# A hybrid encoder layer on one core: scheduling priority of the first group's output projection, and the buffer of the last input rows

## The chip, the cores and the metric

One NeuronCore of a Trainium2 chip runs the whole kernel. The metric is the device time of one execution in microseconds (us), and what is compared is the median of several executions. In the profile PE is the matmul engine (TensorE), DVE is VectorE, ACT is ScalarE, POOL is GpSimd and SP is the engine that issues nearly all DMAs. The granted clock of PE is given as a share of full speed: 1.00 is 2.4 GHz and 0.50 is 1.2 GHz.

## The reference

One layer for 1024 prompt rows and 64 sample rows, D = 1024, so 1088 columns in the kernel's transposed layout:

```
h  = RMSNorm(x) @ W_in
x += W_out @ concat[ConformerConv, ForgettingAttn, HGRN2, StickBreaking]
x += MemoryCrossAttn(RMSNorm(x), mem K/V)
x += SquaredReLU-MLP(RMSNorm(x))
y  = RMSNorm(x)
```

The convolution is a depthwise filter of 31 taps over a gated input, followed by a layer norm over its 256 channels and a SiLU. Each mixer gives 256 of the 1024 channels that W_out takes in.

## The kernel before

Every product is made from three matmuls: both factors are split into a high part (`wh`, `ap` written by ACT) and a low part (`wl`, `ap` written by DVE), and high x high, high x low and low x high are added in PSUM (helper line L71; ACT's helper is L74, DVE's split is L171).

**Start.** x comes in nine row tiles (`TT`: eight of 128 prompt rows and one of 64 sample rows), is transposed on PE (`px`, L282) and split, and the rms factor of each column is broadcast into `rb` (products `pr`). Columns are worked in three chunks of 512, 256 and 320. The nine tiles `xt0` to `xt8` wait in SBUF: the first seven have buffers of their own in pool `xa`, and `xt7` and `xt8` borrow buffers of pool `att`, by naming the tag of a later tile. Two tiles with the same tag share buffers, so the later tile's first write waits until the last reader of the earlier one is done. Before the change `xt8` takes the tag `kT` (one buffer). `kT` is also the tile into which DVE writes the first projection, the keys of the stick-breaking attention: `kT<-pm,rb` (L441), one write for each chunk; the values go to `vT` (L447). Their transposes back are `pn` (L365).

**Middle.** Work is written as generators ("lanes": projections, two attentions, convolution, HGRN) that are recorded in turns; each piece carries a priority, and a scheduler orders the instructions of each engine by priority (a smaller number goes first) and by what is ready. The order is fixed when the program is built; at run time each engine runs its list in order and waits where an operand is missing. The priorities are PR_PROJ < PR_ATT < PR_HGRN < PR_CONV < PR_MM < PR_END. The convolution is the filler of DVE: each tap is one DVE instruction (L794, `y<-ext,cwT,y`). Behind its last taps comes its epilogue, in two halves of 183 columns: sums over channels on PE (`pme`), subtraction (L816), squares on ACT (`sq`), sums of squares on PE (`pva`), the rsqrt chain, scale (L825, L826), SiLU (L830), and the write of the result to DRAM (`mix_d<-y`, L832 to L835).

**End of the mixers.** The output projection is `dense_add` (L1107 on; products `pa`): for each of 8 row tiles m of W_out, 8 terms k, three matmuls for each term; then DVE adds the sum to x (L1120). PSUM pool `ps1` has three buffers and the weight pool two. Group 0 is columns 0 to 511 and group 1 is columns 512 to 1087, in two PSUM pieces of 320 and 256. The inputs are the mixers' results, read back from DRAM and split (`split_mix`, L1035: `mix<-mix_d` for group 0, `aq<-mix_d` for group 1). The convolution gives the terms k = 0 and 1, and its last columns belong to group 1 alone. Group 1 takes its terms in the order `MIX = (2, 3, 4, 5, 6, 7, 0, 1)`. After group 0 come `rms_stats` (`pr`) and `rms_apply` (L1096) for the memory attention. All of this is recorded with `tc.cur_priority = PR_END` (L1033), behind every lane.

Of the kernel before, what the change touches and what calls it, by code (L numbers as in the profile page):

```python
# [8 lines left out]
F32 = mybir.dt.float32  # L9
# [8 lines left out]
P = 128  # L18
D = 1024
# [3 lines left out]
T = SP + SS  # L23
# [15 lines left out]
P_COST = 18.0  # L39
PROJ_ORDER = "sb0 h0 sb1 ff cv fox0 h1 fox1 kv".split()  # L40

PR_PROJ, PR_ATT, PR_HGRN, PR_CONV, PR_MM, PR_END = (i * 10 ** 6 for i in (1, 2, 3, 4, 5, 10))


class Need:
# [7 lines left out]
def kernel(ctx: ExitStack, tc: tile.TileContext, *args):  # L53
# [16 lines left out]
    def mm(out, lhsT, rhs, start, stop, **kw):  # L70
        nc.tensor.matmul(out, lhsT=lhsT, rhs=rhs, start=start, stop=stop, **kw)  # L71

    def act(out, in_, func, **kw):
        nc.scalar.activation(out=out, in_=in_, func=func, **kw)  # L74
# [35 lines left out]
    for m in LEVELS[1:]:  # L110
        nb = 64 // m
        f = const.tile([P, nb], F32, name=f"lf{m}", tag="lvlf", bufs=1)
# [27 lines left out]
    def rstd_chain(pool, n, mean_sq, tag, scale=1.0, parts=P, out=None, tiles=None):  # L140

        tags = [tag + c for c in "vyt"] if isinstance(tag, str) else tag
        tags = [dict(tag=g) if isinstance(g, str) else dict(zip(("tag", "bufs"), g)) for g in tags]
        if tiles:
            v, y, t = tiles[0][:, :n], out, tiles[1][:, :n]
        else:
            v, y, t = (out if c == "y" and out is not None else pool.tile([P, n], F32, name="rs" + c, **g)[:parts]
                       for c, g in zip("vyt", tags))
        V.tensor_scalar(out=v, in0=mean_sq, scalar1=scale, scalar2=EPS, op0=ALU.mult, op1=ALU.add)
        act(y, v, AF.Ln)  # L150
        act(y, y, AF.Exp, scale=-0.5)
        V.tensor_tensor(out=t, in0=y, in1=y, op=ALU.mult)
        V.scalar_tensor_tensor(out=t, in0=t, scalar=-0.5, in1=v, op0=ALU.mult, op1=ALU.mult)
        V.scalar_tensor_tensor(out=y, in0=t, scalar=1.5, in1=y, op0=ALU.add, op1=ALU.mult)
        return y
# [21 lines left out]
    def fetch_w(src, r0, kt, c0, cols=P):  # L177
        raw = wp.tile([P, KD, P], F32, name="wr", tag="wr")[:, :kt, :cols]
        nc.sync.dma_start(out=raw, in_=src[r0:r0 + kt * P, c0:c0 + cols].rearrange("(k p) c -> p k c", p=P))
        return raw  # L180
# [51 lines left out]
    def h_at(k, t0, n):  # L232
        g = 0 if t0 < 512 else 1
        t0 -= GR[g][0]
        return hx[g][k][0][:, t0:t0 + n], hx[g][k][1][:, t0:t0 + n]
# [5 lines left out]
    att = mx.enter_context(tc.tile_pool(name="att", bufs=2))  # L241
    wk = mx.enter_context(tc.tile_pool(name="wk", bufs=2))
    rb = wk.tile([P, T], F32, name="rb", tag="rb", bufs=1)
    with ExitStack() as pa:
        xa = pa.enter_context(tc.tile_pool(name="xa", bufs=1))
        ps_a = pa.enter_context(tc.tile_pool(name="ps_a", bufs=4, space=PSUM))
        ss = xa.tile([P, 9], F32, name="ss")
        V.memset(ss, 0.0)
        junk = att.tile([P, 2, D], BF16, name="junk", tag="vn")
        xt = []  # L250
        for i, (t0, n) in enumerate(TT):
            xt.append((att.tile([P, T], F32, name=f"xt{i}", tag=("vn", "kT")[i - 7], bufs=(2, 1)[i - 7])[:, :D] if i >= 7 else
                       xa.tile([P, D], F32, name=f"xt{i}")))
            nc.sync.dma_start(out=xt[i][:n], in_=x_prompt[t0:t0 + n] if i < 8 else x_sample)
            if i in (3, 6):
                c = (C_SK, C_SV)[i // 3 - 1]
                early[c] = fetch_w(w_in, 0, KD, c)

        def stats(c0, cn, tiles):
            for i in tiles:  # L260
                n = TT[i][1]
                if i % 2:
                    V.tensor_tensor_reduce(out=junk[:n, 1], in0=xt[i][:n], in1=xt[i][:n], scale=1.0, scalar=0.0,
                                           op0=ALU.mult, op1=ALU.add, accum_out=ss[:n, i:i + 1])
                else:
                    act(junk[:n, 0], xt[i][:n], AF.Square, accum_out=ss[:n, i:i + 1])
            r = rstd_chain(xa, len(tiles), ss[:, tiles[0]:tiles[0] + len(tiles)], "ra", scale=1.0 / D)
            pr = ps_a.tile([P, 512], F32, name="pr", tag="pr", bufs=1)
            for j, i in enumerate(tiles):
                n = TT[i][1]  # L270
                dg = xa.tile([P, P], F32, name="dg", tag="dg", bufs=2)
                V.tensor_scalar(out=dg[:n, :n], in0=ident[:n, :n], scalar1=r[:n, j:j + 1], scalar2=None, op0=ALU.mult)
                mm(pr[:, j * P:j * P + n], ones[:n], dg[:n, :n], True, True)
            act(rb[:, c0:c0 + cn], pr[:, :cn], AF.Copy)

        for c0, cn in CH:
            tiles = [i for i, (t0, n) in enumerate(TT) if c0 <= t0 < c0 + cn]
            for k in range(KD):
                px = ps_a.tile([P, 512], F32, name="px", tag="px")
                for i in tiles:  # L280
                    t0, n = TT[i]
                    nc.tensor.transpose(px[:, t0 - c0:t0 - c0 + n], xt[i][:n, k * P:(k + 1) * P], ident[:n, :n])  # L282
                hi, lo = h_at(k, c0, cn)
                act(hi, px[:, :cn], AF.Identity, scale=g_mix[:, k:k + 1])
                V.scalar_tensor_tensor(out=lo, in0=px[:, :cn], scalar=g_mix[:, k:k + 1], in1=hi.bitcast(F32),
                                       op0=ALU.mult, op1=ALU.subtract)
                xs = xa.tile([P, 512], F32, name="xs", tag="xs", bufs=4)
                if k % 2:
                    V.tensor_copy(out=xs[:, :cn], in_=px[:, :cn])
                else:  # L290
                    act(xs[:, :cn], px[:, :cn], AF.Copy)
                nc.sync.dma_start(out=xT_d[:, k, c0:c0 + cn], in_=xs[:, :cn])
            stats(c0, cn, tiles)
# [722 lines left out]
    while lanes:  # L1016
# [13 lines left out]
            ln.need = y.key  # L1030
        else:
            ln.t += y * ln.rate
    tc.cur_priority = PR_END  # L1033

    def split_mix(k, src, t0, n, which):  # L1035
        nc.sync.dma_start(out=src, in_=mix_d[k][:, t0:t0 + n])
# [19 lines left out]
    def unit(tag, dt=F32):  # L1056
        return units[tag].tile([P, 576], dt, name=tag, tag=tag)
# [7 lines left out]
    def wide():  # L1065
        return unit("aq")
# [11 lines left out]
    def rms_stats(g, psum, tag, tiles=None, keep=False, s2=None):  # L1078

        if not s2:  # L1080
            for k in range(KD):
                s2 = add_square(g, k, s2, wide())
        rr = unit("tm")
        for c0, cn in GR[g][2]:
            ps = psum.tile([P, 512], F32, name="pr", tag=tag)
            mm(ps[:, :cn], ones, s2[:, c0:c0 + cn], True, True)
            v, t = tiles or (unit("tm"), unit("tm"))
            rstd_chain(None, cn, ps[:, :cn], "xxx", scale=1.0 / D, out=rr[:, c0:c0 + cn], tiles=(v, t))
            if keep:
                V.tensor_tensor(out=t[:, :cn], in0=v[:, :cn], in1=rr[:, c0:c0 + cn], op=ALU.mult)  # L1090
                nc.sync.dma_start(out=rms_d[:, c0:c0 + cn], in_=t[:, :cn])
        return rr
# [7 lines left out]
    def rms_apply(g, gains, rr, which, over=False):  # L1100

        dst = [pair(which) for _ in range(KD)]
        for c0, cn in GR[g][2]:
            for k in range(KD):
                hf = normed(g, k, gains, rr, c0, cn, xT[g][k] if over else None)
                split(dst[k][0][:, c0:c0 + cn], dst[k][1][:, c0:c0 + cn], hf[:, :cn])
        return dst  # L1107

    def dense_add(g, src, r0, kt, a, psum, ahead=None, store=False, after=None, order=None):

        t0, n, _ = GR[g]
        for m in (0, 4, 1, 5, 2, 6, 3, 7) if after else range(KD):
            w = load_w(src, r0, kt, m * P)
            if ahead:
                ahead(m)
            for c0, cn in GR[g][2]:
                ps = psum.tile([P, 512], F32, name="pa", tag="mm")
                mm3(ps[:, :cn], w, lambda k: (a[k][0][:, c0:c0 + cn], a[k][1][:, c0:c0 + cn]), kt, order=order)
                xs = xT[g][m][:, c0:c0 + cn]
                V.tensor_tensor(out=xs, in0=xs, in1=ps[:, :cn], op=ALU.add)  # L1120
            if store:
                nc.sync.dma_start(out=x2_d[m][:, t0:t0 + n], in_=xT[g][m])
            if after:
                tc.cur_priority += 600
                after(m)
                tc.cur_priority -= 600
# [3 lines left out]
    with ExitStack() as pm_:  # L1130
# [94 lines left out]

        MIX = (2, 3, 4, 5, 6, 7, 0, 1)
        dense_add(0, w_out, 0, KD, mix[0], ps1, ahead)
        h2 = rms_apply(0, g_mem, rms_stats(0, ps2, "sc"), 0)
        dense_add(1, w_out, 0, KD, mix[1], ps1, lambda m: load_x(1, m), order=MIX)
        for g in range(2):  # L1230
# [321 lines left out]
```

## Time and profile before

| | |
|---|---|
| median of 3 runs | 1765.38 us (1765.11 to 1768.04) |
| the profiled execution | 1760.05 us, span 1758.3 us, mean granted PE clock 0.991 |
| busy | PE 1694.8, DVE 1172.1, ACT 791.4, POOL 94.1 us |
| chain of work that ended last | PE 75%, DVE 15%, ACT 4%, DMA 3%, issue 2% |

Read the busy times first, then the chain, to see which engine bounds the span; then the stretches around the two edits. The columns of each view are given with its rows below. "[9.11 <-DVE cvo L805]" behind a row means that the engine was idle for 9.11 us before it, and that the instruction that released it was DVE's write of `cvo`.

### The profile page before, as it was taken

The page shows a single profiled execution, that of the slowest core. Times are in us where ns is not written, and L with a number is a line of the kernel's source. Part 1 is how long each engine was busy: PE and PEld are TensorE (multiplying, and loading weights), DVE is VectorE, ACT ScalarE, POOL GpSimd, SP SyncE. Part 2 cuts the span into 40 slices and gives each one's busy share as a digit, 9 for nine tenths or more (in the row PEclk, how much of TensorE's full clock was granted, in tenths as well). Part 3 has the DMA queues.
Part 4 walks back from the last instruction along what each step waited for, and adds up shares of the span by engine and source line. Part 5 has one row for each costly group of instructions (what it writes and reads, how often), then busy time and mean ns, then how long its engine had stood idle before and what let it go on. Part 6 is the DMA issues. An engine that isn't in the chain of part 4 may idle for free.

```text
span 1758.3 us, 29395 instructions
## 1 busy us (share of the span) xinstructions
PE 1694.8 (96%) x11379; PEld 1504.8 (86%) x11379; DVE 1172.1 (67%) x2231; ACT 791.4 (45%) x1614; POOL 94.1 (5%) x201
## 2 busy tenths in 40 slices
PE   6999999999989979999999999999999999999997
PEld 4987768787777768988899989999999999999987
DVE  6266789988986897667777696555556444444435
ACT  6265657547447855346456363433334212122213
POOL 3021111101120200000000000000000000000000
PEclk9999999999999989999999999999999999999999
DMA  8521332242237348232522343333335722332112
GB/s 256 142 80 33 111 87 88 71 123 76 71 95 215 111 140 254 73 97 67 156 78 73 101 124 99 99 106 99 101 105 203 266 94 87 99 100 74 37 37 102
DMA packets 233195, 194.70 MB, mean 111 GB/s; under 512 B 17502, under 2 KB 199711, under 8 KB 233055
## 3 DMA queue, kind: packets, MB, share of 16 engines
q1 hardware_dynamic: 232639, 192.54, 35.6%
q8 instruction: 90, 1.47, 0.4%
q14 instruction: 50, 0.41, 0.1%
q10 hardware_dynamic: 160, 0.26, 0.0%
q0 software_dynamic: 256, 0.01, 0.0%
HBM read 137.96 MB, written 53.72 MB: 109 GB/s over the span
## 4 chain that ended last, share of the span: by engine, by line
PE 75%; DVE 15%; ACT 4%; DMA 3%; issue 2%; POOL 0%; SPq 0%; DVEq 0%; POOLq 0%; ACTq 0%
PE pz L71 24%; PE pw L71 15%; PE pm L71 11%; PE pa L71 9%; PE pq L71 5%; PE z L71 2%; DVE y L794 2%; PE pmo L71 2%; PE pms L71 1%; PE po L71 1%; PE pt L517 1%; PE pv L71 1%; DVE wl L171 1%; DVE hsc L934 1%; DVE sba L494 1%
## 5 line engine op out<-in xcount | busy, mean ns | idle before, releaser
L74 ACT ACTIVATE wh<-wr 128x1024 fp32r<-128x1024 f32 (+1 forms) x179 | 161.4, 909 | 439.6 <-PE pz L71 195.2
L171 DVE TENSOR_TENSOR wl<-wr,wh 128x1024 fp32r<-128x1024 f32 (+1 forms) x179 | 184.3, 1036 | 63.8 <-ACT wh L74 62.5
L71 PE MATMUL pw<-ap,wh 128*128 128x512 f32 x720 | 223.3, 391 | 1.0 <-DVE xt L1120 0.6
L71 PE MATMUL pz<-ap,wh 128*128 128x288 f32 x988 | 198.3, 294 | 0.0
L71 PE MATMUL pa<-ap,wh 128*128 128x256 f32 (+2 forms) x768 | 187.0, 332 | 2.1 <-DVE xt L1120 2.1
L71 PE MATMUL pm<-hx,wh 128*128 128x512 f32 (+1 forms) x640 | 176.6, 363 | 2.1 <-ACT wh L74 1.4
L71 PEld LDWEIGHTS pz<-ap,wh 128*128 128x128 f32 x988 | 161.3, 188 | 4.6
L71 PE MATMUL pm<-ap,wh 128*128 128x256 f32 (+1 forms) x768 | 164.7, 307 | 0.0
L71 PEld LDWEIGHTS pw<-ap,wh 128*128 128x128 f32 x720 | 130.0, 188 | 23.5 <-issue 0.8
L71 PE MATMUL pz<-ap,wl 128*128 128x288 f32 x494 | 145.4, 294 | 0.0
L71 PEld LDWEIGHTS pa<-ap,wh 128*128 128x128 f32 x768 | 132.3, 191 | 12.5 <-DVE xt L1120 2.4
L71 PE MATMUL pw<-ap,wl 128*128 128x512 f32 x360 | 140.3, 390 | 0.0
L71 PEld LDWEIGHTS pm<-hx,wh 128*128 128x128 f32 x640 | 110.2, 192 | 20.6 <-ACT wh L74 2.2
L71 PEld LDWEIGHTS pm<-ap,wh 128*128 128x128 f32 x768 | 123.8, 191 | 4.2 <-issue 1.7
L71 PE MATMUL pa<-ap,wl 128*128 128x512 f32 (+2 forms) x384 | 127.2, 332 | 0.1
L1349 DVE TENSOR_TENSOR xt<-xt,pz 128x576 f32<-128x576 f32 x56 | 42.2, 753 | 115.6 <-PE pz L71 108.8
L71 PE MATMUL pm<-ap,wl 128*128 128x256 f32 (+1 forms) x384 | 114.0, 297 | 0.0
L71 PE MATMUL pm<-hx,wl 128*128 128x512 f32 (+1 forms) x320 | 112.7, 352 | 0.1
L794 DVE SCALAR_TENSOR_TENSOR y<-ext,cwT,y 128x376 f32<-128x376 f32 (+1 forms) x180 | 100.9, 604 | 0.3
L1349 DVE TENSOR_TENSOR xt<-xt,pw 128x512 f32<-128x512 f32 (+2 forms) x80 | 51.0, 638 | 69.8 <-PE pw L71 67.6
L71 PE MATMUL pq<-ap,wh 128*128 128x512 f32 (+2 forms) x384 | 93.0, 331 | 0.0
L71 PEld LDWEIGHTS pz<-ap,wl 128*128 128x128 f32 x494 | 92.7, 188 | 0.0
(385 smaller groups left out, 3572.9 us busy)
## 6 DMA issues: line engine op xcount, KB each, us to landing
wr<-in_w_up_dram SPq DMA_DIRECT2D x32, 512.0 KB, 4.1
wr<-in_w_down_dram SPq DMA_DIRECT2D x32, 512.0 KB, 3.5
wr<-in_w_in_dram SPq DMA_DIRECT2D x24, 512.0 KB, 4.3
hid_d<-ap SPq DMA_DIRECT2D x32, 288.0 KB, 2.4
aq<-hid_d SPq DMA_DIRECT2D x32, 288.0 KB, 3.7
wr<-in_w_out_dram SPq DMA_DIRECT2D x16, 512.0 KB, 4.2
wr<-in_w_mq_dram SPq DMA_DIRECT2D x16, 512.0 KB, 3.8
wr<-in_w_mo_dram SPq DMA_DIRECT2D x32, 256.0 KB, 2.8
```

The lines of the kernel that those rows point to most:

```text
L71: nc.tensor.matmul(out, lhsT=lhsT, rhs=rhs, start=start, stop=stop, **kw)
L74: nc.scalar.activation(out=out, in_=in_, func=func, **kw)
L171: V.tensor_tensor(out=lo, in0=src, in1=hi.bitcast(F32), op=ALU.subtract)
L494: V.tensor_tensor_scan(out=v[:, ::-1], data0=z[:, n - 1:0:-1], data1=v[:, ::-1], initial=-NEG, op0=ALU.add, op1=ALU.subtract)
L517: nc.tensor.transpose(ps[:w, j - jb], p[:, j * P:j * P + w], ident)
L794: V.scalar_tensor_tensor(out=y, in0=ext[:, j:j + n], scalar=cwT[:, ct, j:j + 1], in1=y, op0=ALU.mult, op1=ALU.add)
L934: V.copy_predicated(sc[r, s_at:s_at + ng, :, r].rearrange("p g h (c w) -> p (g h) c w", w=2 * m)[:, :, :, m:], lvl[m][r, par * nb:(par + 1 ...
L1349: eng.tensor_tensor(out=out, in0=a, in1=b, op=ALU.add)
```

## The change

A new priority PR_OUT stands between PR_HGRN and PR_CONV. The loads and splits of the mixers' results, the weight loads of the first projection and `dense_add(0)` itself are recorded at PR_OUT; after `dense_add(0)` the priority goes back to PR_END. And `xt8` takes the tag `q2` (one buffer, used later by the stacked queries of the stick-breaking attention) in the place of `kT`. Lines below the edits move by one or two (L441 becomes L442, L794 L795, L1120 L1121).

```diff
-PR_PROJ, PR_ATT, PR_HGRN, PR_CONV, PR_MM, PR_END = (i * 10 ** 6 for i in (1, 2, 3, 4, 5, 10))
+PR_PROJ, PR_ATT, PR_HGRN, PR_OUT, PR_CONV, PR_MM, PR_END = (i * 10 ** 6 for i in (1, 2, 3, 4, 5, 6, 10))
...
-            xt.append((att.tile([P, T], F32, name=f"xt{i}", tag=("vn", "kT")[i - 7], bufs=(2, 1)[i - 7])[:, :D] if i >= 7 else
-                       xa.tile([P, D], F32, name=f"xt{i}")))
+            xt.append(att.tile([P, T], F32, name="xt7", tag="vn")[:, :D] if i == 7 else
+                      att.tile([P, 2, T], F32, name="xt8", tag="q2", bufs=1)[:, 0, :D] if i == 8 else
+                      xa.tile([P, D], F32, name=f"xt{i}"))
...
-    tc.cur_priority = PR_END
+    tc.cur_priority = PR_OUT
...
         dense_add(0, w_out, 0, KD, mix[0], ps1, ahead)
+        tc.cur_priority = PR_END
         h2 = rms_apply(0, g_mem, rms_stats(0, ps2, "sc"), 0)
```

What this does to the lists of the engines is seen at three places. First, PE where the output projection begins, before the change (`pv` belongs to the last attention, `pa` is dense_add(0), `pme` is the convolution's first sum):

```order
2340 L71 MATMUL pv<-aT,vn 64x128 x5
2341 L71 MATMUL pa<-ap,wh 128x512 x4
2342 L71 MATMUL pme<-y_4800,ones 128x183
2343 L71 MATMUL pme<-y_4816,ones 128x183
2344 L71 MATMUL pa<-ap,wl 128x512
2345 L71 MATMUL pa<-ap,wh 128x512 x2
2346 L71 MATMUL pa<-ap,wl 128x512
2347 L71 MATMUL pva<-sq_5331,ones 128x183
2348 L71 MATMUL pva<-sq_5332,ones 128x183
```

After the change the same sums stand on PE behind the last product of dense_add(0), among the first ones of dense_add(1) (`pa` of 320 columns):

```order
2467 L71 MATMUL pa<-ap,wh 128x512 x2
2468 L71 MATMUL pa<-ap,wl 128x512
2469 L71 MATMUL pme<-y_4800,ones 128x183
2470 L71 MATMUL pme<-y_4816,ones 128x183
2471 L71 MATMUL pa<-ap,wh 128x320 x2
2472 L71 MATMUL pa<-ap,wl 128x320
2473 L71 MATMUL pa<-ap,wh 128x320 x2
2474 L71 MATMUL pa<-ap,wl 128x320
2475 L71 MATMUL pa<-ap,wh 128x320
2476 L71 MATMUL pva<-sq_5331,ones 128x183
2477 L71 MATMUL pva<-sq_5332,ones 128x183
```

All 192 matmuls of dense_add(0) now stand ahead of the convolution's epilogue; the second half's `pme` and `pva` follow at 2482 to 2492.

Second, DVE at the start of that epilogue, after the change (the adds of dense_add(0) are `xt<-xt,pa`):

```order
1014 L1121 TENSOR_TENSOR xt<-xt,pa 128x512
1015 L171 TENSOR_TENSOR wl<-wr,wh 128x1024
1016 L1121 TENSOR_TENSOR xt<-xt,pa 128x512
1017 L817 SCALAR_TENSOR_TENSOR y_4800<-pme,y_4800 128x183
1018 L817 SCALAR_TENSOR_TENSOR y_4816<-pme,y_4816 128x183
1019 L171 TENSOR_TENSOR wl<-wr,wh 128x1024
1020 L149 TENSOR_SCALAR rs<-pva 128x183
```

The epilogue begins behind the last of the eight adds; the taps themselves end at row 1008, between the fourth add and the fifth. Of the instructions between row 1017 and the epilogue's end at row 1045 only row 1019 is not the convolution's.

Third, DVE at the start of the program, before the change and then after it (`ap<-px` and `xs` belong to the transposes of x):

```order
64 L289 COPY xs<-px 128x320
65 L272 TENSOR_SCALAR dg<-ident,rsy 64x64
66 L441 TENSOR_TENSOR kT<-pm,rb 128x512
67 L171 TENSOR_TENSOR kl<-kT,kh 128x512
68 L769 MEMSET ext_3684 128x30
```

```order
45 L286 SCALAR_TENSOR_TENSOR ap<-px,g_mix,ap 128x320
46 L152 TENSOR_TENSOR rst<-rsy 128x2
47 L442 TENSOR_TENSOR kT<-pm,rb 128x512
48 L153 SCALAR_TENSOR_TENSOR rst<-rst,rsv 128x2
49 L448 TENSOR_TENSOR vT<-pm,rb 128x512
```

The first write of `kT` moves from behind the last of x's transposes to ahead of most of the last chunk's. On PE the transposes `pn<-ident,kT` and the products of the second chunk follow it:

```order
98 L283 MATMUL px<-ident,xt_240 128x64
99 L366 MATMUL pn<-ident,kT 128x128 x4
100 L71 MATMUL pm<-ap,wh 128x256 x2
101 L71 MATMUL pm<-ap,wl 128x256
102 L71 MATMUL pm<-ap,wh 128x256 x2
103 L71 MATMUL pm<-ap,wl 128x256
```

Three of the eight `px` of the last chunk now stand behind these products. From PE's instruction 234 to 3095 and from DVE's 88 to 829 the two programs' lists are the same.

## Rows read from the trace of the kernel before

**Rows 1.** The page, part 1: busy us (share of the span) xinstructions of each engine.
```profile
PE 1694.8 (96%) x11379; PEld 1504.8 (86%) x11379; DVE 1172.1 (67%) x2231; ACT 791.4 (45%) x1614; POOL 94.1 (5%) x201
```

**Rows 2.** The page, part 4: the chain that ended last, by engine.
```profile
PE 75%; DVE 15%; ACT 4%; DMA 3%; issue 2%; POOL 0%; SPq 0%; DVEq 0%; POOLq 0%; ACTq 0%
```

**Rows 3.** Stretches: us, busy of PE, PEld, DVE, ACT, POOL; clock, DMA share, GB/s.
```profile
36.00:44.00 8.00, 5.48 (x31) 3.63 (x29) 7.00 (x21) 5.55 (x14) 0.00 (x0) 0.94 0.58 192
44.00:50.00 6.00, 5.47 (x26) 5.09 (x25) 2.03 (x5) 2.15 (x4) 3.03 (x5) 0.51 0.52 151
...
640.00:660.00 20.00, 10.75 (x69) 8.50 (x69) 19.68 (x39) 5.62 (x13) 0.00 (x0) 0.74 0.48 154
```

**Rows 4.** Timeline of PE where the projection begins: start, us, instruction, [idle before].
```profile
643.60 1.20 PE L71 MATMUL pa<-ap,wh 128*128 128x512 f32 x4
653.90 1.59 PE L71 MATMUL pme<-y,ones 128*128 128x183 f32 x4 [9.11 <-DVE cvo L805]
...
659.28 0.78 PE L71 MATMUL pme<-y,ones 128*128 128x183 f32 x4
...
665.13 0.61 PE L71 MATMUL pa<-ap,wh 128*128 128x512 f32 x2
...
665.81 0.61 PE L71 MATMUL pa<-ap,wh 128*128 128x512 f32 x2
```

**Rows 5.** Timeline of DVE: the last taps and the convolution's epilogue.
```profile
641.37 11.82 DVE L794 SCALAR_TENSOR_TENSOR y<-ext,cwT,y 128x366 f32<-128x366 f32 x23
...
666.46 0.34 DVE L152 TENSOR_TENSOR rs<-sq 128x183 f32<-128x183 f32 x1
...
670.24 0.65 DVE L826 TENSOR_SCALAR y<-y,cvec 128x183 f32<-128x183 f32 x2
...
673.73 0.60 DVE L830 TENSOR_TENSOR y<-y,sq 128x183 f32<-128x183 f32 x2
```

**Rows 6.** Timeline of ACT: root and sigmoid of the epilogue, then a split of the last load.
```profile
658.76 0.36 ACT L74 ACTIVATE sq<-rs 128x183 f32<-128x183 f32 x1 [1.72 <-DVE rs L149]
...
662.73 0.70 ACT L74 ACTIVATE sq<-y 128x183 f32<-128x183 f32 x2 [0.79 <-DVE y L826]
663.33 1.08 ACT L74 ACTIVATE sq<-sq 128x183 f32<-128x183 f32 x4
...
680.64 0.67 ACT L74 ACTIVATE ap<-aq 128x576 fp32r<-128x576 f32 x1
```

**Rows 7.** Timeline of SP's queue: the loads behind the epilogue's writes.
```profile
676.97 0.79 SPq L1036 DMA_DIRECT2D aq<-mix_d  x2
```

**Rows 8.** The DMA view: issues, KB each, median us from issue to landing.
```profile
aq<-mix_d SPq DMA_DIRECT2D x8, 288.0 KB, 3.6
```

**Rows 9.** Timeline of PE in dense_add(1): tiles of 320 columns.
```profile
701.70 0.46 PE L71 MATMUL pa<-ap,wh 128*128 128x320 f32 x2
...
702.14 0.46 PE L71 MATMUL pa<-ap,wh 128*128 128x320 f32 x2
```

**Rows 10.** Timeline of PE at the start of the program.
```profile
36.16 0.38 PE L282 MATMUL px<-ident,xt 128*128 128x128 f32 x2
36.38 0.61 PE L71 MATMUL pr<-dg,ones 128*128 128x128 f32 x4
36.92 1.99 PE L282 MATMUL px<-ident,xt 64*128 64x64 f32 x10
...
40.69 1.21 PE L282 MATMUL px<-ident,xt 128*128 128x128 f32 x6 [0.95 <-ACT xs L74]
43.47 1.41 PE L71 MATMUL pr<-dg,ones 128*128 128x128 f32 x4 [1.57 <-DVE dg L272]
...
50.63 0.40 PE L71 MATMUL pm<-ap,wh 128*128 128x256 f32 x2
...
50.99 0.40 PE L71 MATMUL pm<-ap,wh 128*128 128x256 f32 x2
```

**Rows 11.** Timeline of DVE at the start of the program.
```profile
43.89 0.67 DVE L441 TENSOR_TENSOR kT<-pm,rb 128x512 f32<-128x512 f32 x1
```

## The prediction

> **What bounds the kernel now.** I read the busy times first: PE is busy for 1694.8 of 1758.3 us, DVE for 1172.1 [rows 1]. The chain that ended last runs through PE for 75% and DVE for 15% [rows 2]. So the kernel gets shorter only where PE idles or runs at half clock, some 60 us in all, and the next views are stretches with both columns side by side. Two of them belong to the two edits. Between 640 and 660 us PE is busy for 10.75 of 20 us at a clock of 0.74, while DVE is full with 19.68 [rows 3]. Between 36 and 50 us PE is busy for 5.48 of 8 and then 5.47 of 6, the latter at 0.51 [rows 3]. The timelines say what ended each wait. At 643.60 PE starts the output projection with four matmuls, then idles for 9.11 us until DVE has written `cvo` [rows 4]: next in its list stands the convolution's `pme`, DVE is working through 23 taps in 11.82 us [rows 5], and PE cannot pass over an instruction. In the early stretch there are waits of 0.95 and 1.57 us for the evacuation and scaling of x [rows 10], and the first `kT` is written only at 43.89 [rows 11], with most of PE's products in its list behind it.
>
> I work the sum against the profiled execution, 1760.05 us: its span and 1.75 us around it. It lies 5.3 us below the median of the runs, so I carry the difference, not the level, to 1765.38. A measurement of this kernel tells 0.2% from no change, 3.5 us.
>
> **The change, edit B (`xt8` in tag `q2`).** No instruction is added or removed; a false dependency goes. `kT<-pm` moves up in DVE's list, and on PE 36 to 48 products of 256 columns come to stand among the transposes on which it waited. The stretch to judge runs from 36.16, PE's first transpose after the first chunk's values, to 50.63, from where products of 256 columns go at full speed, three in 0.36 us [rows 10]. Up to 50.20, one triple earlier, are 14.0 us. They hold 21 transposes `px`, 10 broadcasts `pr`, 4 `pc`, 8 `pn`, and 12 products of 256 columns. Four `pr` took 0.54 us from start to start [rows 10], 0.13 each, so 43 x 0.13 = 5.6 us; 12 products take 4 x 0.36 = 1.4 us. The content at full clock is 7.0 us and the loss 7.0 us: 3.05 us of idle time (2.52 + 0.53 from the busy columns [rows 3]), the rest half clock and waits inside the transposes (ten `px` took until the next `pr`, 1.9 us, where 1.3 would do). The wait for `xs` on ACT (0.95 us) is not about `kT`; I keep it. Gain 7.0 - 0.95 = **6.0 us**. The bounds: 7.0 if nothing is left; 2.1 if only idle time goes and the half clock stays. I take the value near the top, since products now fill the places of the waits, and the half clock stands only behind the stretch where PE was mostly idle (the granted clock is 0.94 over 36 to 44 and 0.51 after [rows 3]).
>
> What hides the rest: `k_d<-kh` moves ahead of seven writes of `xT_d` in SP's queue; nobody waits for those writes before the output projection, so I cost it at nothing. The buffer `q2` has no other reader that early. From PE's instruction 234 to 3095 the lists are the same, so all engines run the same program that much earlier, and the gain is carried to the output projection.
>
> **Edit A (priority PR_OUT).** What goes: PE's 9.11 us. All 192 matmuls of dense_add(0) now stand ahead of `pme`, and its splits and weights ahead of the last taps on DVE; the taps fill DVE's gaps beside PE's products (64 threes at 0.68 us [rows 4], 43.5 us). What comes: the epilogue starts when those products end; call that T. I build it from its own rows. First half: `pme` 0.78 [rows 4], subtraction 0.60, squares 0.70, `pva` 0.78, first rsqrt step 0.34, root on ACT 2 x 0.36 [rows 6], three steps on DVE of 0.34, two scalings of some 0.60 and 0.65, sigmoid 0.70 + 1.08 [rows 6], two products of 0.60 [rows 5]: 9.2 us. The second half's sums run beside it; behind it stand three steps, scaling, sigmoid and two products again, 5.2 us. The last `y` is at T + 14.4. In the trace the last `y` ends at 674.33 and the load that needs it is issued at 676.97 [rows 5, 7], 2.64 us for the write; the load takes 3.6 [rows 8] and ACT's split 0.67 [rows 6]. So the terms k = 0 and 1 are ready at **T + 21.3**.
>
> What has PE to do until then? Three PSUM buffers, so k = 2 to 7 of three tiles: 36 matmuls of 320 columns at 0.44 for three [rows 9], 5.3 us; 18 of 256 at 0.36, 2.2 us; and four pairs `pme`, `pva` of 0.78, 3.1 us. Together 10.5 us. Then PE waits 21.3 - 10.5 = 10.8 us. The half clock behind such a wait is paid before and after alike, and cancels. Edit A is 10.8 - 9.1 = **+1.7 us**: the wait isn't removed but moved from the taps to the epilogue, which no longer has dense_add(0)'s products beside it.
>
> On the two transfers in that chain the Trainium skill, DMA: Bandwidth & Descriptors, section Latency and other measured facts, gives each DMA a fixed cost of about 2 us, most of it the receipt from memory; by that estimate write and load would take 4.0 us in the place of the 6.2 of the rows, edit A would be -0.5 and the kernel end at 1758.9 us.
>
> Bounds of A: above, the epilogue lasts as long as in the trace, from 653.90 to 674.33, 20.4 us, though there DVE also made splits and adds between its steps: +7.7. Below, the steps hand over without gaps and a transfer lands early: -1.9. I take the built value, since only one foreign instruction stands among the epilogue's on DVE now.
>
> Behind the wait SP now issues `vr` and `kr` ahead of the weights of group 1's third row tile, and ACT splits them ahead of that tile's `wh`. PE has 24 matmuls of 256 columns and the rest of three tiles before it needs them, some 5 us, which covers two loads that overlap; if that cover is gone, PE waits about 2 us more.
>
> **Sum.** -6.0 + 1.7 = -4.3 us: 1755.8 for an execution like the profiled one, **1761.1 us** for the median. That is 0.24%, just past the bound of 0.2%, so part of the likeliest case falls within it.
>
> **The rivals.**
> 1. *The seam closes.* The convolution's epilogue is covered and PE doesn't wait: -6.0 - 9.1 gives 1750.3 us. For it speaks that DVE gets rid of its taps beside dense_add(0). Against it the list: `pme` stands behind the last product, and 10.5 us of work face a chain of 21.3. Chance 0.06.
> 2. *The new wait is longer than the old: slower.* Place: the last step of the first row tiles of dense_add(1). The epilogue runs as slowly as in the trace (+6.0), and the weights of the third tile come late (+2.0): A is +9.7, the sum +3.7, 1769.1 us. It decides from where k = 0 is ready: beyond T + 25.6 the sum changes its sign, beyond T + 29.1 it is slower by 0.2%. For it: the epilogue of the trace took 20.4 us. Against: what lay between its steps is gone. Chance 0.10.
> 3. *B doesn't arrive.* The early 6 us are lost to something that doesn't move with PE, a transfer or the chain of HGRN, before 640 us: 1765.4 + 1.7 = 1767.1, which is no change. For it: DVE is at two thirds and the chain passes through it [rows 1, 2]. Against: the lists are the same and nearly all starts hang on PE. Chance 0.13.
>
> **How the numbers follow.** The forecast has 0.71. It spreads over 1757 to 1765 by the bounds of B and A; two thirds of it, 0.47, lie more than 3.5 us below 1765.4, and 0.24 within. Faster: 0.47 + 0.06 = 0.53. Slower: 0.09 of rival 2 and 0.01 of rival 3, 0.10. Same: the rest, 0.37. The range reaches from 1756.5 (B -7.0, A -1.9) to 1768.0 (near rival 3, B at -4 with A at +6.6); rival 1 and the upper part of rival 2, with the tails of the forecast, are left out.
>
> **What would show it.** In the profile after, the first `kT<-pm` stands near 35 us, PE is busy throughout 36 to 56 but for about 1 us, at full clock, and the first product of 512 columns of the queries, starts 6 us earlier. The four `pa` that preceded the 9.11 us are followed by more `pa`; dense_add(0) ends about 43.5 us after its start; then `pme`, and a wait of some 11 us ended by ACT or DVE's split of `aq`, with clock 0.5 at its end. The forecast is wrong on A if that wait is under 7 or above 16 us, on B if the start of dense_add(0) moves by less than 3 us.

## The result and the profile after

The changed kernel's four runs took 1753.96 to 1756.11 us, median 1755.3. The four runs of the kernel before that were counted with them lie at 1765.11 to 1768.04, median 1766.14: 10.8 us or 0.6% faster, ratio 0.9937 with an interval of 0.9919 to 0.9954. The forecast was 1761.1 us, a gain of 4.3, with a range from 1756.5. The sign was right; the size was not.

One thing must be known to read this: executions of the kernel before scatter by some 9 us. Beside the later experiments it ran 18 and 21 times more, from 1759.1 to 1767.8, with medians of 1764.45 and 1763.4 us, and against the latter the changed kernel, timed again, was 8.4 us faster (1754.97; ratio 0.9958, interval 0.9945 to 0.9970). So some 2.4 of the first 10.8 us may be scatter of the four runs it was held against. Both intervals together allow 8 to 10 us.

Busy times after, in the page's first part (before: [rows 1]): PE takes 4.2 us less for the same work, and the other 2.0 us of the gain in span (1758.3 to 1752.1) are idle time.

```profile
span 1752.1 us, 29387 instructions
PE 1690.6 (96%) x11366; PEld 1502.2 (86%) x11379; DVE 1172.5 (67%) x2231; ACT 791.4 (45%) x1614; POOL 95.0 (5%) x201
```

**Edit B's place.** Stretches of the kernel after (us, busy of PE, PEld, DVE, ACT, POOL, granted clock, DMA share, GB/s), beside [rows 3]:

```profile
36.00:44.00 8.00, 8.00 (x57) 6.53 (x58) 6.25 (x17) 6.42 (x16) 0.00 (x0) 1.00 0.62 199
44.00:50.00 6.00, 6.00 (x48) 5.74 (x47) 2.57 (x11) 1.15 (x3) 0.27 (x1) 1.00 0.63 196
50.00:58.00 8.00, 6.68 (x47) 6.17 (x47) 3.30 (x7) 2.81 (x6) 2.77 (x5) 1.00 0.38 97
...
680.00:700.00 20.00, 12.80 (x82) 11.95 (x81) 12.17 (x33) 10.20 (x29) 0.00 (x0) 0.91 0.28 80
700.00:720.00 20.00, 17.96 (x112) 17.04 (x113) 16.65 (x27) 12.94 (x21) 0.00 (x0) 0.83 0.47 138
720.00:740.00 20.00, 19.17 (x144) 18.91 (x143) 16.92 (x27) 8.41 (x12) 0.00 (x0) 1.00 0.32 93
```

From 36 to 50 us PE is busy throughout at full clock, where before it was busy for 10.95 of 14 us and the clock fell to 0.51. The timeline of PE there:

```profile
35.57 2.30 PE L283 MATMUL px<-ident,xt 128*128 128x128 f32 x12
37.80 0.66 PE L366 MATMUL pn<-ident,kT 128*128 128x128 f32 x4
38.21 0.48 PE L71 MATMUL pm<-ap,wh 128*128 128x256 f32 x2
...
53.40 0.24 PE L753 MATMUL pcw<-ident,cw 31*128 31x31 f32 x1 [1.32 <-DMA cw<-in_conv_w_dram]
```

and the first `kT` on DVE:

```profile
34.63 0.69 DVE L442 TENSOR_TENSOR kT<-pm,rb 128x512 f32<-128x512 f32 x1
```

`kT` is written at 34.63 us (before 43.89, [rows 11]), and the products of 256 columns start at 38.21. One wait is new: `pcw`, a transpose of the convolution's weights, comes so much earlier that its load has not landed, and PE waits 1.32 us for it.

**Edit A's place.** PE from the first product of dense_add(0), beside [rows 4]:

```profile
638.90 0.73 PE L71 MATMUL pa<-ap,wh 128*128 128x512 f32 x2
639.47 0.39 PE L71 MATMUL pa<-ap,wl 128*128 128x512 f32 x1
...
682.55 0.78 PE L71 MATMUL pme<-y,ones 128*128 128x183 f32 x4
...
701.56 1.43 PE L71 MATMUL pa<-ap,wh 128*128 128x320 f32 x4 [8.76 <-ACT ap L74]
...
703.74 0.85 PE L71 MATMUL pa<-ap,wh 128*128 128x320 f32 x2 [0.48 <-ACT ap L74]
...
728.08 0.50 PE L71 MATMUL pa<-ap,wh 128*128 128x256 f32 x2 [0.83 <-DVE xt L1121]
```

The wait of 9.11 us at the taps is gone, and dense_add(0) runs through in 43.65 us. But in place of it PE waits 8.76 and 0.48 us for ACT's split of the convolution's terms. The clock pays for it as before: 0.91 and 0.83 over the 40 us around it, 10.4 us at half clock, as many as the 0.74 over 20 us of [rows 3] gives. What ACT waits for is seen in the chain of the epilogue. On DVE, its first and last steps:

```profile
683.37 0.60 DVE L817 SCALAR_TENSOR_TENSOR y<-pme,y 128x183 f32<-128x183 f32 x2
...
695.69 0.61 DVE L831 TENSOR_TENSOR y<-y,sq 128x183 f32<-128x183 f32 x2 [0.16 <-ACT sq L74]
```

On SP, the last write and the load that needs it:

```profile
697.39 0.43 SPq L836 DMA_DIRECT2D mix_d<-y  x1
698.05 1.25 SPq L1037 DMA_DIRECT2D aq<-mix_d  x2
```

On ACT, the two splits that PE waits for, of the terms k = 0 and then k = 1:

```profile
700.83 0.68 ACT L74 ACTIVATE ap<-aq 128x576 fp32r<-128x576 f32 x1 [2.83 <-DMA aq<-mix_d]
...
703.00 0.68 ACT L74 ACTIVATE ap<-aq 128x576 fp32r<-128x576 f32 x1 [0.97 <-DMA aq<-mix_d]
```

From `pme` at 682.55 (T) the last `y` takes 13.75 us, the first load is issued 1.75 us behind it, and ACT starts 2.78 us after that: the first term is split at T + 19.0. The second load is issued 0.93 us after the first, at 698.98, and lands 4.0 us later: the second term is split at T + 21.1. In between PE works on the products of the first.

### The profile page after: what moved, and what is told of

Read it like the earlier page. It is cut to its first block, busy times and chain, and to the rows that moved or that the text cites. A ratio compares the mean times of both kernels' runs of the same rounds, so it can differ in the third digit from the quotient of the medians.

```text
span 1752.1 us, 29387 instructions
## 1 busy us (share of the span) xinstructions
PE 1690.6 (96%) x11366; PEld 1502.2 (86%) x11379; DVE 1172.5 (67%) x2231; ACT 791.4 (45%) x1614; POOL 95.0 (5%) x201
## 4 chain that ended last, share of the span: by engine, by line
PE 60%; DVE 4%; DMA 1%; ACT 1%; issue 1%; DVEq 0%; SPq 0%; ACTq 0%
PE pz L71 24%; PE pw L71 16%; PE pa L71 9%; PE pq L71 4%; PE pm L71 2%; PE pmo L71 2%; PE pms L71 1%; PE z L71 1%; DVE wl L171 1%; PE pv L71 1%; DMA wr<-in_w_up_dram 1%; PE pt L518 0%; PE pmt L1182 0%; ACT wh L74 0%; DVE ap L171 0%
## 5 line engine op out<-in xcount | busy, mean ns | idle before, releaser
L171 DVE TENSOR_TENSOR wl<-wr,wh 128x1024 fp32r<-128x1024 f32 (+1 forms) x179 | 184.9, 1039 | 65.4 <-ACT wh L74 64.4
L71 PE MATMUL pa<-ap,wh 128*128 128x256 f32 (+2 forms) x768 | 187.7, 332 | 10.1 <-ACT ap L74 9.2
L71 PE MATMUL pm<-hx,wl 128*128 128x512 f32 (+1 forms) x320 | 112.5, 351 | 0.2 <-DVE wl L171 0.2
L795 DVE SCALAR_TENSOR_TENSOR y<-ext,cwT,y 128x376 f32<-128x376 f32 (+1 forms) x180 | 101.6, 608 | 0.4
```

Of the source, the lines that this page charges most:

```text
L171: V.tensor_tensor(out=lo, in0=src, in1=hi.bitcast(F32), op=ALU.subtract)
L795: V.scalar_tensor_tensor(out=y, in0=ext[:, j:j + n], scalar=cwT[:, ct, j:j + 1], in1=y, op0=ALU.mult, op1=ALU.add)
```

## The experiments

All eight kernels were profiled, two of them twice, and two traces of one kernel differ by some us for reasons of their own. So the span is cut into four stretches: the start, up to a common instruction of PE, the weight load that stands at 90.6 us in the first trace; the mixers, from there to the first `pa`; the projection, from there to the first `pq`; and the rest, up to PE's last instruction (the 9.2 to 9.5 us of the span behind it are left out). The borders were read from the timelines of PE. e1 to e4 ran on one chip and e5 to e8 on another, each group beside the kernel before, to which its ratios are taken.

| execution, us | start | mixers | projection | rest |
|---|---|---|---|---|
| before | 90.6 | 553.0 | 113.9 | 991.5 |
| before again (e1) | 90.0 | 558.4 | 112.7 | 992.4 |
| before, rms later (e8) | 91.2 | 556.0 | 110.5 | 992.4 |
| priority alone (e2) | 94.7 | 555.2 | 112.5 | 991.8 |
| xt8 alone (e3) | 87.5 | 554.7 | 113.6 | 991.2 |
| reads only (e7) | 85.1 | 554.6 | 114.6 | 992.2 |
| changed | 85.7 | 553.2 | 111.4 | 992.5 |
| changed again (e6) | 85.8 | 557.1 | 111.0 | 991.5 |
| split after m = 4 (e4) | 84.9 | 555.1 | 115.2 | 991.2 |
| split, rms later (e5) | 87.3 | 553.5 | 105.1 | 991.9 |

**e1, the kernel before again.** No edit.

> The kernel before, unchanged, for a second trace. Its profiled execution took 1760.05 us, its other runs 1765.1 to 1768.0; the changed kernel's four runs lie at 1754.0 to 1756.1, the profiled one among them. Theory 1 (some executions of before have a wait that the first trace doesn't show): this one takes 1764 to 1768 us, and against the first trace 4 to 8 us more stand at one or two places, the rest being equal. Theory 2 (the difference is spread): every stretch is longer in proportion, 0.3%, by a lower granted clock than 0.991. Theory 3 (the first trace is the rule): it takes 1759 to 1761 us again.

It took 1764.59 us, so theory 3 falls: the first trace was one of the quicker executions. Theory 2 falls too, as the mean clock is 0.991 in both and the stretches are not longer in proportion. Theory 1 holds in so far as most of the difference stands in one stretch, but not as a new wait there. Of the 4.5 us in time the mixers' stretch makes 5.4, and the others give 0.9 back. Two pieces of it in e1 (columns as above):

```profile
500.00:520.00 20.00, 18.31 (x140) 15.79 (x139) 16.30 (x40) 12.60 (x39) 9.69 (x13) 0.91 0.24 73
...
540.00:560.00 20.00, 19.66 (x130) 17.41 (x130) 11.90 (x25) 11.44 (x24) 0.34 (x2) 0.83 0.71 192
```

The same pieces in the first trace of before:

```profile
500.00:520.00 20.00, 18.24 (x150) 15.87 (x149) 17.91 (x43) 11.56 (x37) 10.70 (x15) 1.00 0.28 87
...
540.00:560.00 20.00, 18.81 (x143) 16.94 (x141) 12.95 (x23) 13.51 (x30) 0.34 (x2) 0.96 0.83 229
```

Between 540 and 560 us PE is busier in e1, but at 0.83 and not 0.96, with 130 matmuls in place of 143. The half clock makes a part of the difference: over the whole mixers' stretch PE is busy for 529.89 us in e1 and 527.71 in before, 2.2 us more. The other 3.2 of the 5.4 us are idle time of PE, and what made it is not shown.

**e2, edit A alone.** The lines of PR_OUT, without those of `xt8`.

> Edit A alone: the priority of the first output projection, xt8 staying in kT's buffer. Theory from the two traces: the wait of 9.1 us at the taps becomes one of 8 to 10 us at the last terms of group 1, and the later wait of 2.1 us for the adds goes, so A is worth -1.5 to -3 us against before. The prediction's value was +1.7. Rival: A carries most of the measured 10.8 us, -6 to -9.

1761.11 us over 12 runs, beside 1764.45: ratio 0.9985, interval 0.9976 to 0.9994, so -1.1 to -4.2 us. The theory holds: A is a gain, where the prediction had a loss of 1.7. The wait at the taps is again replaced by one of 8.62 and 0.67 us. The later wait for an add in dense_add(1), which the trace of before has as

```profile
721.06 0.50 PE L71 MATMUL pa<-ap,wh 128*128 128x256 f32 x2 [2.14 <-DVE xt L1120]
```

is 0.82 us here, the last of these rows:

```profile
712.50 1.43 PE L71 MATMUL pa<-ap,wh 128*128 128x320 f32 x4 [8.62 <-ACT ap L74]
714.87 0.85 PE L71 MATMUL pa<-ap,wh 128*128 128x320 f32 x2 [0.67 <-ACT ap L74]
...
740.35 0.50 PE L71 MATMUL pa<-ap,wh 128*128 128x256 f32 x2 [0.82 <-DVE xt L1120]
```

**e3, edit B alone.** The lines of `xt8`, without PR_OUT.

> Edit B alone: xt8 in the buffer of the stacked queries, priorities as before. Theory from the two traces: the lists after the start are the same, the start is 4.7 to 4.9 us shorter and this arrives at the end, -4 to -6 us against before. The prediction's value was -6.0. Rival: the gain is lost before the output projection (0 to -2), or B also removes what makes other executions of before longer (-8 to -10).

1758.71 us, ratio 0.9966, interval 0.9955 to 0.9978: -3.9 to -7.9 us, 5.7 by the medians. Over all traces the start takes 91.6 us without edit B (four) and 86.1 with it (six), 5.6 us less, while the mixers' stretch is the same within its scatter (555.7 and 554.7 us). One of the four, e2's with 94.7, has more half clock than the others; without it the difference is 4.5 us. So the gain is made at the start and arrives.

**e4, the priority back after five row tiles.**

```diff
         for m in (0, 4, 1, 5, 2, 6, 3, 7) if after else range(KD):
+            if early and m == 5:
+                tc.cur_priority = PR_END
             w = load_w(src, r0, kt, m * P)
...
-        dense_add(0, w_out, 0, KD, mix[0], ps1, ahead)
+        dense_add(0, w_out, 0, KD, mix[0], ps1, ahead, early=True)
```

> The changed kernel, but the priority goes back after five of the eight row tiles of dense_add(0) and not after all eight, so that the convolution's epilogue stands beside the last three. Theory (the new wait of 8.8 us is the epilogue's, which has too little work beside it): the wait goes, with the half clock behind it, some 9 to 11 us below the changed kernel, 1744 to 1747 us if that is at 1755. Rival (something else holds PE at the same place, as the loads or DVE's queue): 0 to 4 us below it, with a wait of over 4 us left between 660 and 710 us.

1757.54 us, ratio 0.9967 (0.9955 to 0.9979): no faster than the changed kernel, which has 0.9958 beside before in e6. The first half of the theory held: with three row tiles beside the epilogue the wait for its terms is gone, waits of 0.2 to 0.5 us are left of it. The second half did not. The projection's stretch is 115.2 us, longer than before. PE's longest waits there:

```profile
670.41 0.89 PE L71 MATMUL pva<-sq,ones 128*128 128x183 f32 x4 [1.34 <-ACT sq L74]
...
699.46 0.41 PE L71 MATMUL pa<-ap,wl 128*128 128x320 f32 x1 [0.96 <-DVE wl L171]
...
717.15 0.80 PE L71 MATMUL pa<-ap,wh 128*128 128x256 f32 x2 [2.69 <-DVE xt L1123]
719.44 0.87 PE L71 MATMUL pa<-ap,wh 128*128 128x320 f32 x2 [1.49 <-DVE xt L1123]
721.09 0.64 PE L71 MATMUL pa<-ap,wl 128*128 128x320 f32 x1 [0.78 <-DVE wl L171]
```

The stretches around the last three (columns as above):

```profile
700.00:710.00 10.00, 10.00 (x60) 8.97 (x59) 7.47 (x13) 3.83 (x6) 0.00 (x0) 0.83 0.52 159
710.00:720.00 10.00, 5.82 (x39) 5.20 (x37) 10.00 (x19) 6.65 (x11) 0.00 (x0) 0.85 0.08 26
720.00:730.00 10.00, 9.22 (x48) 8.91 (x47) 4.59 (x6) 0.07 (x2) 0.00 (x0) 0.64 0.48 134
```

DVE is full from 710 to 720 us: it multiplies group 0 by its rms factor and splits it for the memory attention (L1097, L171), one block in its list, and the adds that free PE's three PSUM buffers stand behind it. The wait moved on to that block, and the half clock came with it. The clock is what makes the stretch longer: PE idles for 8.85 us of it, less than the 10.07 of the changed kernel, but is busy for 106.34 us in place of 101.28.

**e8, the kernel before with that block later.** The application is recorded with a priority 300 steps lower, so that its steps stand among the adds:

```diff
-        h2 = rms_apply(0, g_mem, rms_stats(0, ps2, "sc"), 0)
+        rr0 = rms_stats(0, ps2, "sc")
+        p0 = tc.cur_priority
+        tc.cur_priority = p0 + 300
+        h2 = rms_apply(0, g_mem, rr0, 0)
+        tc.cur_priority = p0
```

> The kernel before, with only the application of the rms factor recorded 300 steps later, as in e5. Theory (the wait of 2.1 us for an add in dense_add(1) is due to the block of 11 us on DVE): the wait goes, and the time falls by 2 to 3.5 us, as half clock follows it in some executions only. Rival (the add waits for PE's own pace): the wait stays over 1 us and the time is the same within 1 us.

1761.12 us over 11 runs beside 1763.4, ratio 0.9989 (0.9979 to 0.9998). The trace of before has a wait of 2.14 us for an add at 721.06; here the timeline shows none behind the one at the taps, and the projection's stretch is 110.5 us, the shortest with the old order. By the medians that is 2.3 us, by the ratio 1.9: the theory holds, at its lower end. The block made the wait.

**e5, both: the split after five row tiles and the block later.**

> The kernel of e4 (priority back after five row tiles), with the application of the rms factor to group 0 recorded 300 steps later in priority, so that the adds of dense_add(1) stand among its steps on DVE and not behind a block of them. In e4 the wait for the epilogue went, but between 710 and 722 us PE waited 2.7, 1.5 and 0.8 us for DVE's adds and weights, and the clock was at 0.83, 0.85 and 0.64 over three stretches of 10 us. Theory (the wait moved on to that block): both are gone now, the projection's stretch from its first product to the first `pq`, 115.2 us in e4 and 111.4 in the changed kernel, takes 101 to 104 us, and the time is 7 to 11 us below the changed kernel's, 1744 to 1749. Rival (DVE is simply full there and the wait moves on again): the stretch stays above 108 us.

1749.74 us beside 1763.4: ratio 0.9933, interval 0.9921 to 0.9946, the best of all versions, and 5.2 us below the changed kernel beside it (e6). The theory had 7 to 11 us, and 101 to 104 us for the stretch, which takes 105.1: the mechanism holds, and the gain is smaller than the theory's. The projection's stretch and its busy time:

```profile
640.87:745.93 105.06, 102.00 (x595) 91.14 (x595) 80.78 (x141) 44.13 (x77) 0.00 (x0) 0.98 0.54 167
```

3.1 us of idle time are left in it, where the same stretch of the changed kernel has 10.1:

```profile
638.90:750.25 111.35, 101.28 (x596) 92.20 (x596) 81.13 (x141) 44.68 (x77) 0.00 (x0) 0.95 0.51 158
```

The rest are short waits about 695 us, where the last terms and the weights are split as PE needs them, and a stretch at 0.85 behind them.

**e6, the changed kernel again.** No edit.

> The changed kernel once more, beside the kernel before on this chip. Alone the edits were worth -3.3 us (A) and -5.7 us (B) by their medians. Theory (they add): 1754 to 1757 us, 8 to 10.5 us below before. Rival (together they take away a slow stretch that each alone leaves): 11 us or more below. In its trace the new wait for k = 0 again 8 to 10 us and the stretch from the first product of dense_add(0) to the first `pq` 110.5 to 112.5 us, where before has 112.7 to 113.9.

1754.97 us, 8.4 below before by the medians, 7.4 by the ratio: the edits add (-2.6 and -6.0 by theirs), and the rival of 11 us and more falls. The new wait is 8.79 us.

**e7, only the reads above the taps.**

```diff
-        dense_add(0, w_out, 0, KD, mix[0], ps1, ahead)
         tc.cur_priority = PR_END
+        dense_add(0, w_out, 0, KD, mix[0], ps1, ahead)
```

> The changed kernel, but with the priority put back ahead of dense_add(0): only the loads and splits of group 0's inputs stand above the taps, its products stand behind them as before. Theory (A's gain lies in the projection's stretch, where the later wait of 2.1 us goes): this is as fast as edit B alone, 1757 to 1760 us, with the wait of about 9 us at the taps back. Rival (A's gain comes from the splits that move ahead of the taps in the mixers' last 100 us): as fast as the changed kernel, 1754 to 1756.5.

1759.44 us, ratio 0.9979 (0.9970 to 0.9988), like edit B alone and not like the changed kernel. The wait at the taps is back, longer than before, with 28 taps behind the mixers' last step on DVE where there were 23:

```profile
652.16 1.59 PE L71 MATMUL pme<-y,ones 128*128 128x183 f32 x4 [11.31 <-DVE cvo L806]
```

The later wait for an add is back as well, 2.15 us. Up to the taps PE's list is that of the changed kernel here, and that list differs from before's already from 537 us of the first trace on, where edit A reorders pieces of the mixers; the prediction gave that no price, and it is worth nothing that shows. So moving the reads alone buys nothing; A's gain needs the products ahead of the taps.

## Why the prediction was wrong in size

**What was right.** Edit B: predicted -6.0, measured -5.7 by the runs (-3.9 to -7.9) and -5.6 in the start's stretch, by the mechanism given. Of these 5.6 us, 1.8 are idle time of PE (14.95 to 13.12 on average) and 3.8 busy time, with the granted clock over the start at 0.91 to 0.96 without edit B and 0.98 to 1.00 with it; the prediction had 2.1 and 3.9. That the lists' shift is carried to the end held as well, so rival 3 falls. On A the mechanism was right to the step: dense_add(0) ends after 43.65 us (43.5 predicted), `pme` follows, PE then has work for 10.25 us (10.5), and waits for the split of k = 0. The half clock, which the prediction let cancel, does so on average: PE is busy for 102.0 us of the projection's stretch without edit A (before, e1, e3) and for 101.6 with it (e2, changed, e6). Rival 1, the closed seam, did not happen, and rival 2, a longer wait, neither.

**What failed: the sum of edit A.** It was given as +1.7 us and is -1.8: the projection's stretch takes 113.4 us on average in the three executions with the projection's old order (before, e1, e3) and 111.6 in the three with edit A (e2, changed, e6). By the runs edit A alone is -2.6 (-1.1 to -4.2), which agrees. Two terms make the difference: the end of the epilogue's chain, set too late for the term that PE waits for, and a later wait, which was left out of the sum without a reason.

The first is the chain that ends in T + 21.3, with one end for both terms, k = 0 and 1. For k = 1 it was right, T + 21.1, but PE needs only k = 0 to go on, and that was ready at T + 19.0. Up to there the epilogue took 13.75 us and not 14.4, the step from its last `y` to the load's issue 1.75 and not 2.64, and the load 2.78 and not the median of 3.6. In the trace of before a weight load stands between the write and the read in SP's queue:

```profile
675.94 0.38 SPq L179 DMA_DIRECT2D wr<-in_w_out_dram  x1
```

With that the new wait was 9.24 us in two pieces, one for each term, 0.1 more than the old one, and not 1.7 more. For k = 0 the two transfers took 4.5 us together, nearer to the 4.0 estimated from the fixed cost of about 2 us that the Trainium skill, DMA: Bandwidth & Descriptors, Latency and other measured facts, gives for each DMA, than to the 6.2 of the rows; for k = 1 it was 6.7 us, 4.0 of them in the load alone.

The second was not in the sum at all: the later wait of 2.14 us, at 721.06 in the trace of before. In the changed kernel it is 0.83 us, and 0.82 in e6 and e2. In DVE's list five adds of dense_add(1) now stand ahead of the block of the rms factor, where there were two. Before:

```profile
706.16 0.49 DVE L1120 TENSOR_TENSOR xt<-xt,pa 128x320 f32<-128x320 f32 x1
...
709.54 0.41 DVE L1120 TENSOR_TENSOR xt<-xt,pa 128x256 f32<-128x256 f32 x1
709.87 2.07 DVE L1096 SCALAR_TENSOR_TENSOR tm<-xt,g_mem,tm 128x512 f32<-128x512 f32 x3
```

After:

```profile
705.79 0.48 DVE L1121 TENSOR_TENSOR xt<-xt,pa 128x320 f32<-128x320 f32 x1
...
706.79 0.94 DVE L1121 TENSOR_TENSOR xt<-xt,pa 128x256 f32<-128x256 f32 x2
...
710.97 0.42 DVE L1121 TENSOR_TENSOR xt<-xt,pa 128x256 f32<-128x256 f32 x1 [0.30 <-PE pa L71]
...
714.95 0.48 DVE L1121 TENSOR_TENSOR xt<-xt,pa 128x320 f32<-128x320 f32 x1
...
716.55 2.07 DVE L1097 SCALAR_TENSOR_TENSOR tm<-xt,g_mem,tm 128x512 f32<-128x512 f32 x3
```

e8 shows that the block is what this wait hangs on, and e7 that the wait comes back with the products behind the taps. That it shrinks is worth 1.3 us. The prediction named what comes next after the moved wait only for the weights of the third tile, and did not read the list of DVE through to the next wait.

0.1 for the wait and -1.3 for the later one are -1.2 of the -1.8. The idle time of the projection's stretch says much the same: 11.46 us before, 10.07 and 9.79 in the changed kernel's two traces and 10.11 in e2, so -1.4 to -1.7. The last 0.1 to 0.4 us are PE's busy time, which lies between 101.2 and 102.5 us with either order; values near both ends occur with each, and three traces of each order can't tell such a difference.

**And the level.** -5.6 and -1.8 are 7.4 us, the ratio of the second comparison. The first comparison's 10.8 holds more, from the scatter of before. The prediction named that its profiled execution lay 5.3 us under the median, carried the difference alone, and left the scatter out of its range. With 7.4 us off 1765.4 the changed kernel would stand at 1758.0, inside the range; that the first four runs fell 1.2 us under it takes both, the size of A and the scatter. In what the four runs of before lay higher cannot be said: they have no traces. e1, of 1764.59 us, shows one such difference, in the mixers' stretch, and half clock is a part of it.

## What to carry to other kernels

Here a wait that was removed by moving work ahead came back where the moved-over work was needed, so follow the list to the next two waits and price both: the first returned whole (9.1 us, and 9.0 to 9.3 after) and most of edit A's gain came from the second. Move only as much as covers what is passed over: five of eight row tiles hid the epilogue that all eight had uncovered, and the block on DVE behind it had to be loosened before that paid (1757.5 to 1749.7 us). A borrowed buffer is an edge in the schedule: giving nine tiles' last one another tag was worth more here than the new priority.

## What was not expected

The same program loses different amounts to the half clock from one execution to the next. Between 500 and 560 us, where PE waits often and for 2 us at most, one trace of the kernel before has clocks of 1.00, 0.95 and 0.96 over 20 us each and another 0.91, 1.00 and 0.83, and the mixers' stretch differs by 5.4 us between them, 2.2 of them in PE's busy time. A single trace of such a stretch doesn't give its usual price. And the price of a short wait in clock is not fixed: the 2.14 us in the first trace of before are followed by 0.91 over 20 us, and dense_add(1) takes 56.26 us, while in e1, behind a wait of 2.15, the whole of dense_add(1) runs at 1.00 and takes 54.76.
